# A four-layer encoder trunk whose transposed activations move to another place in each partition's memory

## The chip, the cores and the metric

The kernel runs on one core of one Trainium2 chip. The metric is the device time of one execution in microseconds: lower is better. Before the change the median of three runs is 2669.81 us (2667.91 to 2669.83).

## The reference

A trunk of four post-norm layers over a sequence of 512 tokens of width 1,024. Each layer is a token mixer and a dense feed-forward network (FFN), each followed by a layer norm of `alpha * x + y`. The mixers alternate: multi-head latent attention (MLA) in layers 0 and 3, retention in layer 1, gated linear attention (GLA) in layer 2.

```python
def swiglu_ffn(x, w_in, w_out):
    gate, up = jnp.split(x @ w_in, 2, axis=-1)
    return (jax.nn.silu(gate) * up) @ w_out

for i in range(DEPTH):                       # DEPTH = 4
    y = (mla_mixer, retention_mixer, gla_mixer)[i % 3](x, ...)
    x = layer_norm(DEEPNORM_ALPHA * x + y, ln_g[i, 0], ln_b[i, 0])
    x = layer_norm(DEEPNORM_ALPHA * x + swiglu_ffn(x, ffn_w_in[i], ffn_w_out[i]), ln_g[i, 1], ln_b[i, 1])
```

Everything is float32. `w_in` of the FFN is 1,024 x 5,632 and `w_out` 2,816 x 1,024, so nearly all work is in products of the activations with weights that are read once.

## The kernel before

**A product is three matmuls.** Every operand is kept as two parts, high and low (`split`, lines 99 to 102: ScalarE copies the high part in the rounded type fp32r, VectorE subtracts to get the low part). `mm3` (lines 124 to 128) then issues hi x hi, hi x lo and lo x hi into one accumulator in PSUM. In `mm(out, s, m)` the first operand `s` is stationary (128 x 128, loaded into the array ahead of the matmul) and the second `m` is moving (up to 512 columns). The profile names both, the moving one first: `ps<-xh,whi` streams `xh` past a block of `whi`.

**The transposed activations.** `xh` and `xl` are two tiles of 128 partitions x 8 x 512 floats (16,384 bytes in each partition), the high and low part of x with features on the partitions. `x_to_xT` (lines 151 to 161) fills them from the activations `xt` by TensorE transposes; in MLA the attention's output is put into them too (line 576). They live for the whole program. They are the moving operand where the result has features on the partitions (FFN in, retention's queries and keys, GLA's queries and keys: `proj_f`, line 261) and the stationary operand where it has tokens there (`proj_tile`, line 281, and MLA's output projection, line 616).

**The weights.** `wload` (line 104) brings 512 KB at a time into one of three `wraw` buffers on SyncE's queue; `wsplit` makes `whi` and `wlo` of it, six buffers each of 4,096 bytes per partition.

**All other operands** are blocks of 2,048 bytes per partition from a pool that each mixer and each FFN opens for itself (`phase`, line 76; tags `b`, `v`, `r`). In FFN out and in retention's and GLA's output projections they are stationary and the weights move (`ps<-whi,bh`); in retention's and GLA's inner products both operands come from this pool (`ps<-bh,bl`).

**Where things lie.** Pools are laid out one behind the other in the order in which they are opened, and the tiles in a pool in the order in which they are first asked for, each padded to a multiple of 32 bytes. Each partition of the built program before has, in bytes from its start:

| what | from | to |
|---|---|---|
| DMA scratch and four constants | 0 | 1,152 |
| `cp`: `ident` | 1,152 | 1,664 |
| `cp`: `xh` | 1,664 | 18,048 |
| `cp`: `xl` | 18,048 | 34,432 |
| `cp`: `xt` (four), rotary tables | 34,432 | 55,040 |
| `wp`: `wraw` (three) | 55,040 | 67,328 |
| `wp`: `whi` (six) | 67,328 | 91,904 |
| `wp`: `wlo` (six) | 91,904 | 116,480 |
| `sp`, `lnp` | 116,480 | 125,696 |
| `phase` | 125,696 | 223,136 |

In the GLA mixer's phase a 32-byte tile (`ba`, line 853) stands behind the 35 blocks of tag `b`, so the blocks of tags `v` that follow begin at 197,408.

The framework's planner sets the order of instructions on each engine from the program text, its dependences and its own costs (`issue_after` and `keep_in_program_order` pin a few places); a pool that rotates its buffers makes an instruction wait until the last reader of the buffer is done. The 12 matmuls that close a run of GLA scores are the first of the state updates (line 1092): their moving operand is `v`, a block of tag `v`, and the profile calls it `bh` or `bl` too.

Of the kernel before, what the change touches and what calls it, by code (L numbers as in the profile page):

```python
# [10 lines left out]
F32R = mybir.dt.float32r  # L11
# [5 lines left out]
P = 128  # L17
D = 1024
S = 512
NT = S // P  # L20
KT = D // P
# [29 lines left out]
class Trunk:  # L51
    def __init__(self, tc, ctx, ins, nb=47, nraw=3, nhl=6):
        self.tc, self.nc, self.ins = tc, tc.nc, ins
        nc = tc.nc
        ctx.enter_context(nc.allow_non_contiguous_dma(reason="rows of weights and broadcasts"))
        pool = lambda name, bufs, **k: ctx.enter_context(tc.tile_pool(name=name, bufs=bufs, **k))
        self.cp = pool("cp", 1)
        self.wp = pool("wp", 1)
        self.nb = nb
        self.sp = pool("sp", 8)  # L60
        self.lnp = pool("lnp", 2)
        self.ps_pool = pool("psum", 6, space=bass.MemoryType.PSUM)
        self.nraw, self.nhl = nraw, nhl
        self.relieve = 0
        self.pending = []
        self.waiting = []

        self.ident = self.cp.tile([P, P], F32, name="ident")
        make_identity(nc, self.ident)
        self.xh = self.cp.tile([P, KT, S], F32R, name="xh")  # L70
        self.xl = self.cp.tile([P, KT, S], F32R, name="xl")
        self.xt = [self.cp.tile([P, D], F32, name=f"xt{t}") for t in range(NT)]


# [1118 lines left out]
```

## Time and profile before

| | |
|---|---|
| median of three runs | 2669.81 us |
| the profiled execution | 2668.85 us |
| its span (first to last instruction) | 2667.1 us |
| TensorE matmuls: busy, share, number | 2611.8 us, 98%, 12,996 |
| VectorE | 1416.6 us, 53% |
| ScalarE | 906.0 us, 34% |
| DMA: moved, mean busy share of 16 engines | 230 MB, 28.5% |
| granted TensorE clock, mean | 0.994 of 2.4 GHz |

The busy time of TensorE is the union of its matmuls; they are pipelined, so that two overlap, and a matmul's own duration (some 390 ns for 512 columns) is longer than the distance from its start to the next one's start. How fast TensorE works is read from the starts.

### The profile page before, as it was taken

To read this page: it belongs to the slowest core of one execution; us is meant where nothing else is said; L and a number is where in the kernel's file an instruction comes from. 1 tells how busy PE (TensorE), PEld (TensorE's weight loads), DVE (VectorE), ACT (ScalarE), POOL (GpSimd) and SP (SyncE) were. 2 spreads that over 40 slices of the span, in tenths; PEclk is the share of its full clock that TensorE was granted. 3 is DMA by queue.
4 is the path that set the end of the run, shared out by engine and by line. 5 is a ranking of instruction groups with operands and counts; after the bars stand their busy time and mean duration, and the time that the engine had idled before them with its cause. 6 is when DMAs were issued, how large, how long until landed. Compare 5 with 4: busy or idle time off the path is not lost.

```text
span 2667.1 us, 32309 instructions
## 1 busy us (share of the span) xinstructions
PE 2611.8 (98%) x12996; PEld 2191.9 (82%) x12996; DVE 1416.6 (53%) x2484; ACT 906.0 (34%) x1381; POOL 218.7 (8%) x231
## 2 busy tenths in 40 slices
PE   8999999999999999999999999999999999999998
PEld 6888888887888888888888998888888788888886
DVE  6878433238755548333226888833335586633334
ACT  4752322213333332322213654322212564322211
POOL 3002000001110103000002010100002200100001
PEclk9999999999999999999999999999999999999999
DMA  4212433232223222333223221333322221333321
GB/s 142 72 40 68 127 95 95 95 95 87 79 72 95 88 93 82 103 95 95 95 94 99 75 64 56 107 95 95 95 95 78 67 74 48 101 93 94 94 95 56
DMA packets 294711, 232.35 MB, mean 87 GB/s; under 512 B 21120, under 2 KB 244480, under 8 KB 294560
## 3 DMA queue, kind: packets, MB, share of 16 engines
q1 hardware_dynamic: 294560, 230.28, 28.5%
q8 instruction: 102, 1.67, 0.3%
q14 instruction: 49, 0.40, 0.0%
HBM read 228.15 MB, written 2.10 MB: 86 GB/s over the span
## 4 chain that ended last, share of the span: by engine, by line
PE 84%; DVE 10%; POOL 2%; issue 2%; ACT 2%; DMA 1%; DVEq 0%; SPq 0%; ACTq 0%; POOLq 0%
PE ps L126 27%; PE ps L128 27%; PE ps L127 27%; DVE xt L203 2%; DVE xt L204 1%; PE tp L555 1%; DVE lnst L184 1%; DVE xl L101 1%; PE ps L536 1%; DVE lnu L143 1%; PE ps L535 1%; DVE xt L182 1%; DMA wraw<-in_mla_w_down 0%; PE tp L156 0%; DVE bl L101 0%
## 5 line engine op out<-in xcount | busy, mean ns | idle before, releaser
L100 ACT CAST whi<-wraw 128x1024 fp32r<-128x1024 f32 (+3 forms) x414 | 430.4, 1040 | 1150.9 <-issue 383.9
L101 DVE TENSOR_TENSOR wlo<-wraw,whi 128x1024 fp32r<-128x1024 f32 (+2 forms) x366 | 444.4, 1215 | 674.5 <-ACT whi L100 664.1
L127 PE MATMUL ps<-xl,whi 128*128 128x512 f32 (+1 forms) x1792 | 666.0, 372 | 8.5 <-DVE xl L101 8.5
L126 PE MATMUL ps<-xh,whi 128*128 128x512 f32 (+1 forms) x1792 | 666.3, 372 | 0.0
L128 PE MATMUL ps<-xh,wlo 128*128 128x512 f32 (+1 forms) x1792 | 665.5, 371 | 0.0
L127 PEld LDWEIGHTS ps<-xl,whi 128*128 128x128 f32 x1792 | 338.6, 189 | 72.5 <-DVE xl L101 9.7
L126 PEld LDWEIGHTS ps<-xh,whi 128*128 128x128 f32 x1792 | 338.7, 189 | 63.1 <-issue 0.4
L128 PEld LDWEIGHTS ps<-xh,wlo 128*128 128x128 f32 x1792 | 338.5, 189 | 62.9
L126 PE MATMUL ps<-whi,bh 128*128 128x512 f32 (+1 forms) x960 | 369.4, 385 | 0.2 <-ACT bh L100 0.2
L128 PE MATMUL ps<-whi,bl 128*128 128x512 f32 (+1 forms) x960 | 368.0, 383 | 0.0
L127 PE MATMUL ps<-wlo,bh 128*128 128x512 f32 (+1 forms) x960 | 367.8, 383 | 0.0
L128 PE MATMUL ps<-whi,xl 128*128 128x512 f32 (+3 forms) x752 | 264.8, 352 | 5.3 <-DVE xl L101 5.3
L126 PE MATMUL ps<-whi,xh 128*128 128x512 f32 (+3 forms) x752 | 267.0, 355 | 0.8 <-ACT xh L100 0.8
L127 PE MATMUL ps<-wlo,xh 128*128 128x512 f32 (+3 forms) x752 | 264.3, 351 | 0.1
L101 POOL TENSOR_TENSOR wlo<-wraw,whi 128x1024 fp32r<-128x1024 f32 (+4 forms) x48 | 117.3, 2457 | 1672.1 <-ACT whi L100 1658.8
L126 PEld LDWEIGHTS ps<-whi,bh 128*128 128x128 f32 x960 | 181.0, 189 | 35.6 <-ACT bh L100 1.0
L128 PEld LDWEIGHTS ps<-whi,bl 128*128 128x128 f32 x960 | 180.9, 188 | 35.5 <-DVE bl L101 0.6
L127 PEld LDWEIGHTS ps<-wlo,bh 128*128 128x128 f32 x960 | 180.9, 188 | 34.7
L304 DVE TENSOR_TENSOR b<-ps,b 128x512 f32<-128x512 f32 x88 | 60.9, 692 | 273.5 <-PE ps L128 272.8
L128 PEld LDWEIGHTS ps<-whi,xl 128*128 128x128 f32 x752 | 142.3, 189 | 25.5 <-DVE xl L101 6.6
L126 PEld LDWEIGHTS ps<-whi,xh 128*128 128x128 f32 x752 | 142.5, 189 | 20.5 <-ACT xh L100 1.2
L127 PEld LDWEIGHTS ps<-wlo,xh 128*128 128x128 f32 x752 | 142.6, 190 | 19.0 <-POOL wlo L101 0.4
(220 smaller groups left out, 2780.4 us busy)
## 6 DMA issues: line engine op xcount, KB each, us to landing
wraw<-in_ffn_w_in SPq DMA_DIRECT2D x176, 512.0 KB, 3.8
wraw<-in_ffn_w_out SPq DMA_DIRECT2D x88, 512.0 KB, 3.3
wraw<-in_ret_w_in SPq DMA_DIRECT2D x48, 512.0 KB, 3.8
wraw<-in_gla_w_in SPq DMA_DIRECT2D x22, 512.0 KB, 3.6
wraw<-in_mla_w_o SPq DMA_DIRECT2D x16, 512.0 KB, 3.8
wraw<-in_ret_w_o SPq DMA_DIRECT2D x16, 512.0 KB, 4.8
wraw<-in_mla_w_down SPq DMA_DIRECT2D x8, 512.0 KB, 4.5
wraw<-in_mla_w_ukv SPq DMA_DIRECT2D x8, 512.0 KB, 3.7
```

The costliest lines, as they stand in the source:

```text
L100: a = self.nc.scalar.copy(hi, src)
L101: b = (eng or self.nc.vector).tensor_tensor(lo, src, hi.bitcast(F32), op=ALU.subtract)
L126: mm(out, s[0], m[0], start=start, stop=False)
L127: mm(out, s[0], m[1], start=False, stop=False)
L128: mm(out, s[1], m[0], start=False, stop=stop)
L143: stt(u, y, y, x, op0=ALU.mult, op1=ALU.mult)
L182: nc.vector.scalar_tensor_tensor(x, x, coef, ps, op0=ALU.mult, op1=ALU.add)
L184: nc.vector.bn_stats(self.stats[t][:, half * 6 : half * 6 + 6], x)
L203: nc.vector.scalar_tensor_tensor(x[:, sl], x[:, sl], mv[:, 0:1], self.g[:, sl], op0=ALU.subtract, op1=ALU.mult)
L204: nc.vector.scalar_tensor_tensor(x[:, sl], x[:, sl], r, self.bb[:, sl], op0=ALU.mult, op1=ALU.add)
L304: nc.vector.tensor_tensor(s, pu, s, op=ALU.mult)
L535: nc.tensor.matmul(ps, qr[:, sl], krh, start=False, stop=False)
```

## The change

The two tiles `xh` and `xl` are no longer taken from the pool `cp`, the first that is opened, but from a pool of their own, `xp`, which is opened behind `wp`, `sp` and `lnp` and ahead of the phases' pools. Nothing else in the program text differs.

```diff
@@ Trunk.__init__
         self.sp = pool("sp", 8)
         self.lnp = pool("lnp", 2)
+
+        xp = pool("xp", 1)
+        self.xh = xp.tile([P, KT, S], F32R, name="xh")
+        self.xl = xp.tile([P, KT, S], F32R, name="xl")
         self.ps_pool = pool("psum", 6, space=bass.MemoryType.PSUM)
@@
         make_identity(nc, self.ident)
-        self.xh = self.cp.tile([P, KT, S], F32R, name="xh")
-        self.xl = self.cp.tile([P, KT, S], F32R, name="xl")
         self.xt = [self.cp.tile([P, D], F32, name=f"xt{t}") for t in range(NT)]
```

By the same rule of layout, everything between `xl` and the phases moves down by 32,768 bytes and the two tiles move up by 91,264: `xt` from 1,664, `wraw` from 22,272, `whi` from 34,560 to 59,136, `wlo` from 59,136 to 83,712, `sp` and `lnp` to 92,928, `xh` from 92,928, `xl` from 109,312. The phases' pools begin at 125,696 as before.

## Rows read from the trace of the kernel before

**Rows 1.** The page: busy time of each engine; the chain that ended last, by engine.
```profile
PE 2611.8 (98%) x12996; PEld 2191.9 (82%) x12996; DVE 1416.6 (53%) x2484; ACT 906.0 (34%) x1381; POOL 218.7 (8%) x231
...
PE 84%; DVE 10%; POOL 2%; issue 2%; ACT 2%; DMA 1%; DVEq 0%; SPq 0%; ACTq 0%; POOLq 0%
```

**Rows 2.** Busy time by stretch: start of MLA, FFN in, FFN out of layer 0.
```profile
core 0: us, PE busy (x) PEld busy (x) DVE busy (x) ACT busy (x) POOL busy (x), PEclk, DMA share, GB/s
0.00:60.00 60.00, 50.81 (x263) 43.75 (x263) 35.74 (x59) 27.94 (x57) 23.63 (x67) 1.00 0.51 158
...
263.00:478.00 215.00, 215.00 (x996) 177.52 (x996) 82.98 (x97) 66.87 (x85) 0.00 (x0) 1.00 0.35 103
478.00:600.00 122.00, 122.00 (x538) 100.77 (x538) 35.10 (x45) 23.75 (x24) 4.79 (x2) 1.00 0.30 95
```

**Rows 3.** Matmuls by start and duration (us), FFN in, layer 0: first, 173rd.
```profile
299.81 0.40 PE L128 MATMUL ps<-xh,wlo 128*128 128x512 f32 x1
...
339.79 0.39 PE L126 MATMUL ps<-xh,whi 128*128 128x512 f32 x1
```

**Rows 4.** The same view, FFN in of layer 1: first and 173rd.
```profile
1119.68 0.40 PE L128 MATMUL ps<-xh,wlo 128*128 128x512 f32 x1
...
1159.82 0.40 PE L126 MATMUL ps<-xh,whi 128*128 128x512 f32 x1
```

**Rows 5.** The same view, FFN out of layer 0: first and 178th.
```profile
499.70 0.39 PE L128 MATMUL ps<-whi,bl 128*128 128x512 f32 x1
...
539.82 0.39 PE L128 MATMUL ps<-whi,bl 128*128 128x512 f32 x1
```

**Rows 6.** The same view, retention, both operands of the phase's pool: first, 16th.
```profile
999.72 0.39 PE L128 MATMUL ps<-bh,bl 128*128 128x512 f32 x1
...
1003.12 0.39 PE L128 MATMUL ps<-bh,bl 128*128 128x512 f32 x1
```

**Rows 7.** Matmuls by start, GLA scores: first, 22nd, 34th (the first not of them).
```profile
1628.44 0.28 PE L126 MATMUL ps<-bh 128*128 128x256 f32 x1
...
1630.96 0.28 PE L126 MATMUL ps<-bh 128*128 128x256 f32 x1
...
1632.38 0.40 PE L126 MATMUL ps<-whi,bh 128*128 128x512 f32 x1
```

**Rows 8.** The same view, a GLA projection of 256 columns: first and 40th.
```profile
1614.65 0.28 PE L127 MATMUL ps<-wlo,xh 128*128 128x256 f32 x1
...
1619.27 0.28 PE L127 MATMUL ps<-wlo,xh 128*128 128x256 f32 x1
```

**Rows 9.** Groups by shape (count, busy us, mean ns): 512 columns, by operands.
```profile
L126 PE MATMUL ps<-xh,whi 128*128 128x512 f32 x1408 | 556.0, 395 | 0.0
...
L126 PE MATMUL ps<-whi,bh 128*128 128x512 f32 x896 | 350.6, 391 | 0.2 <-ACT bh L100 0.2
...
L126 PE MATMUL ps<-whi,xh 128*128 128x512 f32 x432 | 172.7, 400 | 0.0
...
L126 PE MATMUL ps<-bh,whi 128*128 128x512 f32 x128 | 51.9, 409 | 0.7 <-ACT bh L434 0.7
...
L126 PE MATMUL ps<-bh,xh 128*128 128x512 f32 x16 | 6.5, 405 | 0.0
```

**Rows 10.** Groups by shape: 256 and 320 columns with `xh`.
```profile
L126 PE MATMUL ps<-xh,whi 128*128 128x256 f32 x384 | 110.3, 287 | 0.0
...
L126 PE MATMUL ps<-whi,xh 128*128 128x256 f32 x224 | 63.8, 285 | 0.0
...
L126 PE MATMUL ps<-whi,xh 128*128 128x320 f32 x64 | 21.1, 330 | 0.8 <-ACT xh L100 0.8
```

**Rows 11.** Transposes by start, eight merged: of `xt`, and of a block of MLA's phase.
```profile
608.94 1.04 PE L156 MATMUL tp<-ident,xt 128*128 128x128 f32 x8
...
180.02 1.03 PE L555 MATMUL tp<-ident,b 128*128 128x128 f32 x8
```

## The prediction

> **What bounds the kernel now.** I read the page first, for which engine sets the end. Matmuls are busy for 2,611.8 of 2,667.1 us, and the chain that ended last is TensorE's to 84% [rows 1]; the next engine, VectorE, is at 53%. So the time is the number of matmuls times the distance from one start to the next, plus a few gaps. Then the stretches: in FFN in and FFN out the matmuls fill all of the 215 and 122 us at a full clock (PEclk 1.00), with DMA busy 0.35 and 0.30, VectorE 83 and 35 us, ScalarE 67 and 24 us [rows 2]. Only the first 60 us leave TensorE idle (50.8 busy).
>
> Nothing is added or removed here, so the one thing to ask is whether a matmul's pace depends on where its operands lie. For that I read starts in the time-ordered view, kind by kind:
> - FFN in, layer 0 (`xh` and `xl` move past weights): 172 steps in 39.98 us, 232.4 ns each [rows 3]. Layer 1: 172 steps in 40.14 us, 233.4 ns [rows 4].
> - FFN out (weights move past blocks of the phase's pool): 177 steps in 40.12 us, 226.7 ns [rows 5].
> - Retention with both operands in the phase's pool: 15 steps in 3.40 us, 226.7 ns [rows 6].
>
> All four have 512 columns, 128 x 128 stationary blocks, and one PSUM bank as target. FFN in and FFN out also bring and split weights at the same rate (24 matmuls to a 512 KB load). What sets the first two apart is the pair `xh`, `xl`, and its place.
>
> **Why the place, and which property of it.** From the table of the layout, take each address modulo 256. `whi`, `wlo` and all blocks of tag `b` begin at a multiple of 256 (67,328 = 263 x 256; 91,904 = 359 x 256; 125,696 = 491 x 256), and so does each row and each slice that these matmuls read. `xh` and `xl` begin 128 behind one (1,664 = 6 x 256 + 128; 18,048 = 70 x 256 + 128). The kernel holds one more case of that sort, far from the start of memory: GLA's `v`, at 197,408 = 771 x 256 + 32. In one run of GLA scores, 21 steps of 256 columns with all operands on multiples take 2.52 us, 120.0 ns each; then the moving operand becomes `v`, and 12 steps take 1.42 us, 118.3 ns [rows 7]. The projections with `xh` at 256 columns step by 4.62 us / 39 = 118.5 ns [rows 8]. So operands off the multiple share a pace that is not the aligned one, whether they lie at 1,664 or at 197,408: 1.5 ns quicker at 256 columns, 6 to 7 ns slower at 512. I take the offset as the cause.
>
> **The change part by part.** `xh` goes to 92,928 = 363 x 256 and `xl` to 109,312 = 427 x 256. Modulo 2,048 both are then 768, as blocks of tag `b` are; and the weights shift by 32,768, which leaves their offsets alone. So each matmul with `xh` or `xl` becomes, in its offsets, one of those that run at 226.7 ns today.
>
> - *512 columns.* There are 3 x (1,408 + 432 + 16) = 5,568 (one of the three lines of `mm3` stands for each kind [rows 9]). The mean of the two paces is 232.9 ns, so 6.24 ns each: -34.7 us. This is what all of them would give.
> - *Runs that don't settle.* The whole of FFN out, with its starts, takes 122.0 us for some 536 matmuls, 227.5 ns, 0.8 above the settled 226.7 [rows 2, 5]. FFN in is one run of 912 a layer, 3,648 in all; the other 1,920 come in short runs, and I charge these the 0.8: +1.5 us.
> - *256 columns.* 3 x (384 + 224) = 1,824 [rows 10], from 118.5 to 120.0 ns [rows 7, 8]: +2.7 us.
> - *320 and 288 columns.* 192 [rows 10] and, from the code, 96. No row shows them with all operands aligned. By the nearest rows they lie between 1.5 ns slower (as 256) and 6.24 quicker (as 512): +0.4 to -1.8 us. I take 0, since the widths lie near 256.
> - *Gain that waits swallow.* At the head of MLA, TensorE waits for weights (9.2 of 60 us idle [rows 2]). The 192 matmuls of the query projection stand there in layers 0 and 3: up to 192 x 6.24 = 1.2 us lost.
> - *Other engines.* ScalarE and VectorE write `xh` and `xl`, DMA writes `wraw`: all at new addresses. The trace has no pair to price this, but cover is large: in FFN in they are busy for 67 and 83 of 215 us, DMA for 0.35 [rows 2]. FFN in shortened by 3% asks 3% more of them. If the cover were gone the gain of that stretch would be lost, nothing more.
> - *Transposes* read `ident` and `xt`. Both are 128 off the multiple and stay so: 0.
>
> Sum: -34.7 + 1.5 + 2.7 + 1.2 = -29.3 us. From the profiled execution's 2,668.85 us that is 2,639.5; it lies 0.96 below the median of the runs, so about 2,640.5 us.
>
> **The Trainium skill speaks against this.** The rows say that the pace goes with the operand's place: 232.4 and 233.4 against 226.7 ns [rows 3 to 5]. The page "SBUF — State Buffer", section "Who interferes with whom", gives TensorE two independent read ports of its own and says that TensorE never waits on anyone; contention exists on VectorE's and GpSimd's shared pair alone. By that rule the home of an operand would be indifferent and the sum 0. The trace does not contradict that no other engine is the disturber, but the two paces need some reason.
>
> **The rivals.**
> 1. *The place is indifferent; it is the use that is slow.* Then `xh` and `xl` keep 232.9 ns wherever they lie: 2,669.8 us. For it: all slow 512-column matmuls have `xh` or `xl`, so use and place cannot be parted at that width. The Trainium skill's page would have it so. Against: as stationary or moving operand, `xh` has the same shape and strides in use as a block of the phase's pool, and `v`, which is not `xh`, leaves the 120.0 ns too [rows 7]. Chance 0.08.
> 2. *The low end of memory is slow, and it reaches past the weights' new home.* `xh` lay below 34,432. If that is why, and the slow part ended before 34,560, the result is my forecast. But reads by TensorE of 34,560 to 67,328 are shown today for transposes alone. Were all of that slow, `whi` (34,560 to 59,136) and two of six `wlo` buffers (to 67,328) would be in it: 2/3 + 1/3 x 1/3 = 7/9 of all products with a weight. FFN in and the like would keep 7/9 of their 34.7 us and gain 7.7; the other 3 x (896 + 128) = 3,072 matmuls with weights [rows 9] would lose 6.24 x 7/9 each, 14.9 us: +7.2 us, 2,677 us. It turns into a loss from a border near 58,000, where `whi` is nearly all inside. Against: eight transposes of `xt`, which lies there now, take 1.04 us, eight of a block of the phase's pool 1.03 [rows 11], and `v` is odd at 197,408. Chance 0.05.
> 3. *Only long runs settle.* If short runs stay uneven, 3,648 x 6.24 = 22.8 us are gained and the four FFNs' 1,152 matmuls of 256 columns lose 1.7: -21 us, 2,649 us. For it: MLA's and GLA's matmuls switch width every few. Against: the short retention run is at 226.7 [rows 6]. Chance 0.08.
>
> **How the numbers follow.** Forecast 0.79, rivals 0.08, 0.05, 0.08. A measurement of this kernel tells some 0.2%, 5.3 us, from no change. Faster: forecast and rival 3, 0.87; within: rival 1, 0.08; slower: rival 2, 0.05. Low end: the full 34.7 us without the losses, 2,634. High end: beyond rival 3 by its own 3 us, 2,652; that leaves out rivals 1 and 2 and some of the forecast's tail.
>
> **What would show it.** Right: FFN in's steps at 226.7 ns in all four layers, the same as FFN out's, unchanged; the 256-column projections at 120.0; `v` still at 118.3; 12,996 matmuls, order as before. Wrong: steps of 232 with `xh` at 92,928 (rival 1); FFN out at over 227 ns, or `ps<-xh,whi` slower than `ps<-xh,wlo` (rival 2); FFN in at 226.7 but retention and MLA not (rival 3). If the planner orders instructions otherwise, the difference is not the place's alone.

## The result, and the profile after

The changed kernel takes 2636.39 us, the median of four runs (2635.14 to 2637.76), against 2668.86 us for four runs of the kernel before (2667.69 to 2669.83): a ratio of 0.988, 95% interval 0.986 to 0.990. It is 32.5 us faster; the forecast was 2640.5 us, 2634 to 2652.

The instructions are the same 32,309, and all but the waits for semaphores, of which a few are recorded some places earlier or later, stand in the same order on every engine; only addresses differ (line numbers are 2 higher behind the edit). So the two traces can be laid side by side row for row. First the page of the changed kernel: TensorE's busy time fell by 33 us, VectorE's and ScalarE's by under 1 us, and the chain is still TensorE's.

```profile
PE 2578.4 (98%) x12996; PEld 2191.5 (83%) x12996; DVE 1416.0 (54%) x2484; ACT 905.5 (34%) x1381; POOL 220.6 (8%) x231
...
PE 85%; DVE 9%; POOL 2%; issue 2%; ACT 2%; DMA 1%; DVEq 0%; SPq 0%; ACTq 0%; POOLq 0%
```

Then the starts, in the time-ordered view (start and duration in us, line, operation, target, moving operand, stationary operand). FFN in of layer 0: the 1st and the 179th matmul of the stretch, 178 steps in 40.34 us, 226.6 ns each, against 232.4 [rows 3].

```profile
299.63 0.39 PE L128 MATMUL ps<-xh,whi 128*128 128x512 f32 x1
...
339.97 0.39 PE L129 MATMUL ps<-xl,whi 128*128 128x512 f32 x1
```

FFN in of layer 1, from 1,109.76 to 1,149.88 us: 177 steps, 226.7 ns, against 233.4 [rows 4]; the table below has all four layers.

FFN out of layer 0: 177 steps in 40.12 us, 226.7 ns, as in [rows 5].

```profile
499.77 0.39 PE L129 MATMUL ps<-wlo,bh 128*128 128x512 f32 x1
...
539.89 0.39 PE L129 MATMUL ps<-wlo,bh 128*128 128x512 f32 x1
```

A GLA projection of 256 columns: 38 steps in 4.56 us, 120.0 ns, against 118.5 [rows 8]. (GLA's `v`, which still lies 32 bytes off, has 11 steps from 1,612.28 to 1,613.57 us, 117.3 ns, against 118.3 [rows 7].)

```profile
1599.83 0.28 PE L128 MATMUL ps<-whi,xh 128*128 128x256 f32 x1
...
1604.39 0.28 PE L130 MATMUL ps<-whi,xl 128*128 128x256 f32 x1
```

The time from the first of FFN in's 912 long-run matmuls to the first of FFN out, read from such starts, and the stretches between, in us (MLA, retention, GLA and MLA each end with the FFN's first matmuls of 256 columns):

| stretch | before | after | difference |
|---|---|---|---|
| MLA, layer 0 | 275.6 | 274.6 | -1.0 |
| FFN in, layer 0 | 211.9 | 206.8 | -5.2 |
| FFN out and retention | 600.9 | 595.7 | -5.2 |
| FFN in, layer 1 | 212.8 | 206.8 | -6.1 |
| FFN out and GLA | 415.0 | 411.6 | -3.5 |
| FFN in, layer 2 | 211.9 | 206.8 | -5.2 |
| FFN out and MLA, layer 3 | 391.1 | 389.3 | -1.8 |
| FFN in, layer 3 | 212.8 | 206.8 | -6.1 |
| FFN out, layer 3 | 119.5 | 119.5 | 0.0 |

FFN in's differences are the change's alone. The stretches with mixers also hold waits on VectorE, and behind a wait TensorE's granted clock sometimes falls for a while from 2.4 to 1.2 GHz. In the stretch of FFN out and GLA TensorE's three longest waits stand at the same places in both kernels: 2.0, 2.3 and 3.6 us before, 1.8, 2.3 and 3.6 us after. What the clock was just behind each of them (columns as in [rows 2]; PEclk is the third figure from the end), before:

```profile
1624.20:1627.20 3.00, 3.00 (x14) 3.00 (x15) 2.88 (x3) 2.98 (x6) 0.00 (x0) 0.50 0.01 3
1651.40:1654.40 3.00, 3.00 (x10) 2.31 (x9) 2.89 (x15) 0.00 (x0) 0.00 (x0) 0.50 0.22 65
1689.00:1692.00 3.00, 3.00 (x16) 3.00 (x15) 2.93 (x10) 0.99 (x2) 0.00 (x0) 0.50 0.14 51
```

and after:

```profile
1606.50:1609.50 3.00, 3.00 (x25) 2.82 (x26) 2.88 (x4) 2.98 (x6) 0.00 (x0) 1.00 0.01 3
1632.00:1635.00 3.00, 3.00 (x17) 2.32 (x16) 2.93 (x19) 0.00 (x0) 0.00 (x0) 1.00 0.39 115
1668.00:1671.00 3.00, 3.00 (x16) 2.92 (x15) 3.00 (x10) 1.17 (x2) 0.00 (x0) 0.50 0.04 5
```

So the clock fell three times before and once after, behind the same waits. Other executions of this stretch, whose places and paces are told further down, show what this is worth: with one fall it takes 411.9 us at the old paces (the pair high and 128 off) and 411.6 or 411.5 at the new ones, with two falls 413.2 at the new ones, with three 415.0 at the old ones. A fall costs some 1.6 us, and of the 3.5 us of this row 0.3 are the change's.

### The profile page after: what moved, and what is told of

Its sections match the earlier page's. It is cut to its first block, busy times and chain, and to the rows that moved or that the text cites. A ratio compares the mean times of both kernels' runs of the same rounds, so it can differ in the third digit from the quotient of the medians.

```text
span 2633.3 us, 32309 instructions
## 1 busy us (share of the span) xinstructions
PE 2578.4 (98%) x12996; PEld 2191.5 (83%) x12996; DVE 1416.0 (54%) x2484; ACT 905.5 (34%) x1381; POOL 220.6 (8%) x231
## 4 chain that ended last, share of the span: by engine, by line
PE 85%; DVE 9%; POOL 2%; issue 2%; ACT 2%; DMA 1%; DVEq 0%; SPq 0%; ACTq 0%; POOLq 0%
PE ps L128 27%; PE ps L130 27%; PE ps L129 27%; DVE xt L205 2%; DVE xt L206 1%; PE tp L557 1%; DVE lnst L186 1%; DVE xl L103 1%; PE ps L538 1%; DVE lnu L145 1%; PE ps L537 1%; DMA wraw<-in_mla_w_down 0%; DVE xt L184 0%; PE tp L158 0%; DVE bl L103 0%
## 5 line engine op out<-in xcount | busy, mean ns | idle before, releaser
L129 PEld LDWEIGHTS ps<-wlo,bh 128*128 128x128 f32 x960 | 180.5, 188 | 34.7
```

The source lines that it names most:

```text
L129: mm(out, s[0], m[1], start=False, stop=False)
```

## The experiments

**Low in memory, but on a multiple of 256.** The kernel before, with one padding tile of 128 bytes on either side of the pair (the `memset` writes its first element).

```diff
+        self.pad0 = self.cp.tile([P, 32], F32, name="pad0")
+        nc.gpsimd.memset(self.pad0[:, :1], 0.0)
         self.xh = self.cp.tile([P, KT, S], F32R, name="xh")
         self.xl = self.cp.tile([P, KT, S], F32R, name="xl")
+        self.pad1 = self.cp.tile([P, 32], F32, name="pad1")
+        nc.gpsimd.memset(self.pad1[:, :1], 0.0)
```

> The kernel before with 128 bytes of padding ahead of xh and 128 behind xl: the pair stays at the low end of memory (1,792 to 34,560) but begins at a multiple of 256; weights and blocks move up by 256 and stay on multiples. If the offset within 256 bytes is the cause: FFN in at 226.7 ns a step, 2636 to 2638 us, as after the change. If the low end of memory is slow: FFN in stays at 232 to 233 ns, 2669 us.

Measured 2640.08 us (2638.31 to 2640.79), ratio 0.989 (0.987 to 0.991). `xh` and `xl` lie at 1,792 to 34,560, and FFN in steps by 40.12 us / 177 = 226.7 ns:

```profile
299.80 0.39 PE L132 MATMUL ps<-xh,wlo 128*128 128x512 f32 x1
...
339.92 0.39 PE L132 MATMUL ps<-xh,wlo 128*128 128x512 f32 x1
```

The low end of memory is not slow: 256 bytes of padding in the old place give FFN in the pace that the move gives it. The whole is 2 us above the 2638 us at which the expectation ended; what makes them was not separated (the next two runs with agreeing operands, on the same chip, took 2637.6 and 2638.0).

**High in memory, but 128 off.** The changed kernel with the same padding around the pair, in `xp`.

```diff
         xp = pool("xp", 1)
+        self.pad0 = xp.tile([P, 32], F32, name="pad0")
+        nc.gpsimd.memset(self.pad0[:, :1], 0.0)
         self.xh = xp.tile([P, KT, S], F32R, name="xh")
         self.xl = xp.tile([P, KT, S], F32R, name="xl")
+        self.pad1 = xp.tile([P, 32], F32, name="pad1")
+        nc.gpsimd.memset(self.pad1[:, :1], 0.0)
```

> The changed kernel with 128 bytes of padding ahead of xh and 128 behind xl: the pair keeps its new home (93,056) but begins 128 bytes behind a multiple of 256, as it did in its old one. Offset theory: FFN in back at 232 to 233 ns a step, 2668 to 2670 us, the whole gain gone. Low-end theory: FFN in at 226.7 ns, 2636 us.

Measured 2669.26 us (2665.80 to 2670.93, ten runs), ratio 0.9996 (0.9987 to 1.0005): the whole gain is gone. FFN in of layer 0 steps by 40.13 us / 172 = 233.3 ns:

```profile
299.81 0.40 PE L132 MATMUL ps<-xh,whi 128*128 128x512 f32 x1
...
339.94 0.40 PE L133 MATMUL ps<-xl,whi 128*128 128x512 f32 x1
```

So the home behind the weights is worth nothing by itself that these runs could tell.

**Everything 128 off.** The kernel before with one padding tile, behind `xl`: the weights (67,456) and the phases' blocks (125,824) now begin 128 bytes behind a multiple of 256, as `xh` and `xl` do.

```diff
         self.xl = self.cp.tile([P, KT, S], F32R, name="xl")
+        self.pad1 = self.cp.tile([P, 32], F32, name="pad1")
+        nc.gpsimd.memset(self.pad1[:, :1], 0.0)
```

> The kernel before with 128 bytes of padding behind xl: now xh, xl, all weights and all blocks of the phases begin 128 bytes behind a multiple of 256 (only v and the transposes' xt differ). If what counts is the distance of an operand from a multiple: all 512-column matmuls at 232 to 233 ns, FFN out too; 3,680 more of them at 6.24 ns, so some 2690 us. If what counts is that the two operands of a matmul differ in their offset: all at 226.7, 2637 us. Low-end theory: as before, 2669 us.

Measured 2637.61 us (2636.72 to 2640.61), ratio 0.988 (0.987 to 0.990). FFN in: 178 steps in 40.35 us, 226.7 ns; FFN out: 177 in 40.12, 226.7 ns.

```profile
299.62 0.39 PE L129 MATMUL ps<-xl,whi 128*128 128x512 f32 x1
...
339.97 0.39 PE L130 MATMUL ps<-xh,wlo 128*128 128x512 f32 x1
...
499.77 0.39 PE L130 MATMUL ps<-whi,bl 128*128 128x512 f32 x1
...
539.89 0.39 PE L130 MATMUL ps<-whi,bl 128*128 128x512 f32 x1
```

This falls against the reason that the prediction gave. No operand need lie on a multiple of 256; the operands need only agree in their distance from one. `xh` and `xl` were slow because they differed from everything that they met.

**256 off.** The changed kernel with 256 bytes ahead of `xh` (the pair and the phases on multiples of 512, the weights 256 behind one).

> The changed kernel with 256 bytes of padding ahead of xh: the pair and the phases' blocks lie at multiples of 512, the weights 256 behind one. If 256 is the step that counts: 2636 us, FFN in and FFN out at 226.7 ns. If it is 512: both FFN in and FFN out mix two offsets (or have one operand off) and step at about 232 to 233 ns, some 2669 to 2690 us.

Measured 2638.01 us (2635.85 to 2641.05), ratio 0.988 (0.987 to 0.990). FFN in steps by 226.7 ns (177 in 40.12 us), so a distance of 256 between the operands is as good as none.

```profile
299.74 0.39 PE L132 MATMUL ps<-xh,wlo 128*128 128x512 f32 x1
...
339.86 0.39 PE L132 MATMUL ps<-xh,wlo 128*128 128x512 f32 x1
```

**The cost by itself.** Behind the changed kernel stand runs of 61 matmuls on one tile of 10,240 floats, in a phase of their own.

```diff
...
+        mv = lambda k, d, n: big[:, (k % 8) * 512 + d // 4 : (k % 8) * 512 + d // 4 + n]
+        st = lambda k, d: big[:, 6144 + (k % 16) * 128 + d // 4 : 6144 + (k % 16) * 128 + d // 4 + P]
+        for name, n, pairs in self.CASES:
+            ps = self.ps_pool.tile([P, 512], F32, tag="ps", name=name)
+            for k in range(self.STEPS):
+                dm, ds = pairs[k % len(pairs)]
+                nc.tensor.matmul(ps[:, :n], st(k, ds), mv(k, dm, n), start=k == 0, stop=k == self.STEPS - 1)
...
+    STEPS = 61
```

> The changed kernel, and behind it 25 runs of 61 matmuls each on one tile of the phase's pool, 128 x 128 stationary blocks; each run fixes how far the moving and the stationary operand begin behind a multiple of 256 bytes. Only the steps between starts in these runs are read. Theory (the two operands of a matmul must agree modulo 256, which the run with all operands 128 off suggests): 226.7 ns at 512 columns for differences 0, 256 and 512 and for both 128 off; 232 to 233 ns for 32, 64, 96, 128, 160, 192, 224, whichever operand is off; 120.0 ns against 118.5 at 256 columns. Rival: what must agree is the moving operand with the stationary block that is loaded for the next matmul while it streams. Two runs part them: alternating pairs (0, 0), (128, 128) agree within each matmul and differ across; pairs (0, 128), (128, 0) differ within and agree across. Theory: 226.7 in the first, 232 to 233 in the second. Rival: the other way round.

The time-ordered view merges each run into one row, under its target's name; the difference of two starts, over 61, is the step. In `s_a` to `s_j` the stationary operand is 0, 32, 64, 96, 128, 160, 192, 224, 256, 512 bytes off; in `m_b` both are 128 off; `x_a` alternates (0, 0) and (128, 128), `x_b` (0, 128) and (128, 0); in `m_a` the moving operand alone is 128 off.

```profile
2648.80 14.00 PE L1169 MATMUL s_a<-probe 128*128 128x512 f32 x61
2662.63 14.39 PE L1169 MATMUL s_b<-probe 128*128 128x512 f32 x61
2676.86 14.40 PE L1169 MATMUL s_c<-probe 128*128 128x512 f32 x61
2691.10 14.44 PE L1169 MATMUL s_d<-probe 128*128 128x512 f32 x61
2705.37 14.33 PE L1169 MATMUL s_e<-probe 128*128 128x512 f32 x61
2719.55 14.40 PE L1169 MATMUL s_f<-probe 128*128 128x512 f32 x61
2733.78 14.14 PE L1169 MATMUL s_g<-probe 128*128 128x512 f32 x61
2747.76 14.39 PE L1169 MATMUL s_h<-probe 128*128 128x512 f32 x61
2761.99 13.99 PE L1169 MATMUL s_i<-probe 128*128 128x512 f32 x61
2775.82 13.99 PE L1169 MATMUL s_j<-probe 128*128 128x512 f32 x61
2789.64 14.38 PE L1169 MATMUL m_a<-probe 128*128 128x512 f32 x61
2803.86 14.02 PE L1169 MATMUL m_b<-probe 128*128 128x512 f32 x61
2817.72 14.10 PE L1169 MATMUL x_a<-probe 128*128 128x512 f32 x61
2831.66 14.19 PE L1169 MATMUL x_b<-probe 128*128 128x512 f32 x61
2845.69 6.92 PE L1169 MATMUL w_as<-probe 128*128 128x128 f32 x61
```

`s_a`, `s_i` and `s_j` step by 13.83 us / 61 = 226.7 ns, `m_b` by 227.2 (its start included). The differences between step by 229.2 (192 off, `s_g`) to 233.9 ns (96 off, `s_d`), and `m_a` by 233.1. So the theory of the agreement modulo 256 holds for constant pairs. On which pair must agree neither view holds: `x_a`, which agrees within each matmul, steps by 228.5 ns, `x_b`, which agrees across, by 230.0. Both cost something, and each less than the constant difference of 128 (`s_e`, 232.5). By the same division (rows not shown) 256 columns give 120.7 ns agreeing and 118.9 with 128 off, 320 columns 146.9 and 146.7, 384 columns 173.4 and 175.9.

**Only `xl` off.** The changed kernel with a padding tile of 128 bytes between `xh` and `xl` and one behind: one of the three matmuls of each product with `xh` and `xl` has operands that differ.

> The changed kernel with 128 bytes of padding between xh and xl and 128 behind xl: xh lies on a multiple of 256 as the weights and blocks do, xl 128 behind one. One of the three matmuls of each product then has operands that differ. If each such matmul costs some 6.2 ns by itself: a third of the 5,568, 11 us of the gain are lost, 2647 us. If a single difference upsets the pace of the whole run: FFN in at 232 to 233 ns and 2668 us. If it is absorbed by its two neighbours: 2637 us.

Measured 2658.91 us (2654.18 to 2662.94), ratio 0.996 (0.995 to 0.998): some two thirds of the gain are lost to a third of the matmuls, between the first two answers, so that none of the three was right. FFN in of layer 0 has the full 233.3 ns (172 steps in 40.13 us); in layer 2 it steps by 40.28 us / 176 = 228.9, with the same addresses and order (in layer 1 by 231.1 and in layer 3 by 233.3; each layer keeps its pace from its first matmul to its last):

```profile
299.81 0.40 PE L133 MATMUL ps<-xl,whi 128*128 128x512 f32 x1
...
339.94 0.39 PE L134 MATMUL ps<-xh,wlo 128*128 128x512 f32 x1
...
1739.63 0.39 PE L134 MATMUL ps<-xh,wlo 128*128 128x512 f32 x1
...
1779.91 0.40 PE L133 MATMUL ps<-xl,whi 128*128 128x512 f32 x1
```

**Mixed runs.** The same set-up with other patterns.

> The changed kernel, and behind it 24 runs of 61 matmuls on one tile, as in the run before; only steps between starts are read. Open from it: alternating pairs that agree within a matmul and differ across stepped by 228.4 ns, those that differ within and agree across by 230.0, and a third of differing matmuls took two thirds of the gain. Theory A (two costs that add, 3.3 ns where a matmul's own operands differ and 1.7 where the moving one and the next stationary differ): every second matmul with an operand 128 off gives 226.7 + 2.5 = 229.2, one in three 228.4, one in six 227.5, one in twelve 227.1; pairs that change every second matmul and agree within, 227.5. Theory B (a difference upsets a rhythm that needs some six agreeing matmuls to settle): one in two, three and six all at 230 to 233, one in twelve some 228.5 to 230; agreeing pairs that change every sixth matmul above 228. Runs of 256 columns with differences of 32 to 224: between 118 and 120 ns if they share one cause with 128; a step under 117 would point to a placement that is better still.

`y_b`, `y_c`, `y_d`, `y_e`: the moving operand 128 off in every second, third, sixth, twelfth matmul, the rest agreeing; `y_a`: the stationary one in every second; `z_a` and `z_b`: agreeing pairs that change every second and every sixth. `q_a` and `q_b`: 256 columns, the stationary operand 32 and 64 off.

```profile
2648.35 14.39 PE L1169 MATMUL y_a<-probe 128*128 128x512 f32 x61
2662.58 14.19 PE L1169 MATMUL y_b<-probe 128*128 128x512 f32 x61
2676.61 14.12 PE L1169 MATMUL y_c<-probe 128*128 128x512 f32 x61
2690.57 14.05 PE L1169 MATMUL y_d<-probe 128*128 128x512 f32 x61
2704.46 14.02 PE L1169 MATMUL y_e<-probe 128*128 128x512 f32 x61
2718.32 14.29 PE L1169 MATMUL z_a<-probe 128*128 128x512 f32 x61
2732.45 14.09 PE L1169 MATMUL z_b<-probe 128*128 128x512 f32 x61
2746.37 14.30 PE L1169 MATMUL z_c<-probe 128*128 128x512 f32 x61
...
2767.72 7.08 PE L1169 MATMUL q_b<-probe 128*128 128x256 f32 x61
2774.64 7.49 PE L1169 MATMUL q_c<-probe 128*128 128x256 f32 x61
```

`y_b` to `y_e` step by 230.0, 228.9, 227.7, 227.2 ns, near theory A; but `y_a` has 233.3 where A says 229.2, and `z_a` 231.6 where A says 227.5. Theory B says 230 to 233 for one in three and one in six, and misses those, though `z_b` is at 228.2, as it foresaw. Both fall. In `y_b` to `y_e` the excess over 226.7 comes to 6 to 7 ns for each matmul whose moving operand is off, with nothing for the others; one stationary operand off (`y_a`) costs twice that. The pairs that change (`x_a`, `x_b`, `z_a`, `z_b`) follow neither figure. `y_c` is the pattern of the run with `xl` off, which in layer 2 had the same 228.9, but in layer 0 233.3. What picks among the paces is not settled.

Five runs (rows not shown) have the moving operand off by itself. 64 off (start 2,825.09, next start 2,839.07) it steps by 229.2 ns, as the stationary one does 192 off; 160 off (2,839.07 to 2,853.34) by 233.9, as the stationary one does 96 off. So what counts is how far the one lies ahead of the other modulo 256.

`q_b` is a find: 6.92 us / 61 = 113.4 ns at 256 columns. The six other differences there give 117.7 to 120.0.

**A placement that might be better still.** The weight buffers are 4,352 bytes each, and a load can begin some bytes into its own. The FFNs' first weights begin 64 in; in the second kernel GLA's of 256 columns begin 192 in as well. A third run repeats the changed kernel on the same chip. The lines that hand the distance down to the buffers are left out here.

```diff
...
-            wg = self.wcols(w_in, 0, KT, f * P, P)
-            wu = self.wcols(w_in, 0, KT, F + f * P, P)
+            wg = self.wcols(w_in, 0, KT, f * P, P, 64)
+            wu = self.wcols(w_in, 0, KT, F + f * P, P, 64)
...
-            ws = [self.proj_w(w, c0, 256, 4) for _, c0, _ in parts]
+            ws = [self.proj_w(w, c0, 256, 4, off=192) for _, c0, _ in parts]
...
-            wv, wr, n = self.proj_w(w, cv, 256, 4), [], 256 + 2 * GLA_RANK
+            wv, wr, n = self.proj_w(w, cv, 256, 4, off=192), [], 256 + 2 * GLA_RANK
```

> The changed kernel once more, beside the two that build on it, so that the three share their runs of the kernel before: 2636 us, give or take 2.

> The changed kernel with weight buffers of 4,352 bytes, and the weights of each FFN's first three blocks of features begin 64 bytes into theirs. They are the stationary operands of 1,152 matmuls of 256 columns whose moving operand stays on a multiple of 256. If the 113.3 ns of the run on one tile hold here against 120.0: 6.7 ns each, 7.7 us at most, less what TensorE then waits for the layer norm before it: 2629 to 2633 us. If the 113.3 ns hang on the single tile or the steady run: 2636 us.

> As the one before, and GLA's weights of 256 columns begin 192 bytes into their buffers: there the weights move and xh, xl are stationary, so that the stationary operand again lies 64 bytes ahead of the moving one modulo 256. 672 more matmuls of 256 columns, 4.5 us at most: 2624 to 2631 us in all if the difference alone decides, 2629 to 2633 if only weights as stationary operand gain.

Measured 2638.28 us for the changed kernel (2636.36 to 2640.49; ratio to before 0.989, 0.987 to 0.991), 2636.03 with the FFNs' weights moved (2633.76 to 2636.80; 0.988, 0.986 to 0.989), 2634.99 with GLA's too (2634.71 to 2635.08; 0.988, 0.986 to 0.989). The steps did what was hoped: in the last kernel 38 steps of a GLA projection take 4.30 us, 113.2 ns.

```profile
1488.40 0.28 PE L131 MATMUL ps<-whi,xh 128*128 128x256 f32 x1
...
1492.70 0.28 PE L133 MATMUL ps<-whi,xl 128*128 128x256 f32 x1
```

But the time did not follow. In the stretch from 1,400 to 1,700 us TensorE's waits are alike to 0.1 us but for one (us in total, times, longest), which in the repeat of the changed kernel reads

```profile
PE tp L1052 <- DVE bl L103: 1.8, 1, 1.8
```

and in the kernel with both:

```profile
PE tp L1055 <- DVE bl L103: 5.0, 3, 3.0
```

The transposes of GLA's keys wait for VectorE 3.2 us longer: TensorE arrives earlier at work that is not ready. The stretch from FFN out to the next FFN in takes 413.2 us in the one and 413.5 in the other. The clock has a part in that: behind the three longest waits of this stretch it fell twice in the first and three times in the second (1.00, 0.52, 0.53 and 0.50, 0.50, 0.51 of 2.4 GHz over 3 us), which is worth some 1.6 us. The longer wait need not be behind the third fall: with the FFNs' weights alone moved, where that wait is 1.8 us as in the first, the clock fell three times too (0.51, 0.51, 0.50). Both expectations that foresaw a gain of 5 us or more missed; the intervals of the three ratios overlap, so that a gain of 3 us is not shown, though all four runs of the last kernel (2635.08 us at most) lie below all four of the changed one (2636.36 at least).

## Why the prediction was right, point by point

**What bounds the kernel** held: with the order unchanged, a quicker step on TensorE became time almost one for one.

**Which property of the place** was right for the sum and wrong in its wording. "So operands off the multiple share a pace that is not the aligned one": the run with everything 128 off shows that being off is harmless. `v` was at 32 against operands at 0, so it fitted both readings, and the text took the narrower one. The step that carried the sum, that each matmul with `xh` becomes one whose operands stand to each other as in [rows 5], was the sound one.

**512 columns, with the runs that don't settle: -34.7 + 1.5 = -33.2 us forecast.** Over all such matmuls whose distance to the next start is under 255 ns (5,523 before, 5,522 after), the mean above 226.7 ns fell from 6.1 to 0.2 ns: about -32.6 us. FFN in alone gave 5.2 + 6.1 + 5.2 + 6.1 = 22.5 us; forecast 3,648 x 6.24 ns = 22.8.

**256 columns: +2.7 us forecast.** Over those whose distance is under 150 ns (1,760 before, 1,731 after) the mean lies 1.1 ns below 120.0 before and 0.1 after: +1.8 us. The term was too large, since the mean before was 118.9 ns and not the 118.5 of the one run that was read.

**320 and 288 columns: 0 taken.** At 320 columns, agreeing and 128 off, the runs by themselves step by 146.9 and 146.7 ns; in the kernels the steps of 288 columns have a mean of 133.1 ns before and 132.6 after, which for 96 is nothing.

**Gain that waits swallow: +1.2 us forecast.** This is the mis-sized term: no stretch shows a loss. MLA of layer 0 got 1.0 us shorter, though the clock fell once there (0.50 from 241.2 to 244.2 us) and not at all before, and FFN out with MLA of layer 3 got 1.8 shorter, where 288 matmuls x 6.24 less 288 x 1.5 would give 1.4 each. GLA's 192 wide matmuls give 1.2 us and its 960 narrow ones take back up to 1.4; the 3.5 us by which that stretch got shorter are the clock's but for 0.3, as told beside the table.

**The sum.** The terms as measured, -32.6 and +1.8, make -30.8 us. The median fell by 32.5. The 1.7 us between are no term of the prediction; runs of one kernel differ by 2 to 3 us, and the profiled execution before had the clock down more often than the one after in the stretch with GLA. What part of the 1.7 us the clock has in the median is not shown.

**The rivals.** That the place is indifferent and the use is slow: fell with FFN in at 226.7 ns. In the first runs on one tile no other engine worked at all (the row below, columns as in [rows 2]: VectorE, ScalarE and GpSimd 0.00 us), and the pace of 512 columns lay between 226.7 and 233.9 ns by how the two operands lie to each other. The Trainium skill's page "SBUF — State Buffer", section "Who interferes with whom", from which that rival followed, gives TensorE two independent read ports and says that TensorE never waits on anyone. The trace agrees in so far as no other engine is needed for the slow pace; it does not bear out that the place of the two operands is indifferent. That the low end is slow: fell with the padded kernel before, 2640 us. That only long runs settle: fell, since retention and FFN out took 5.2 us less together, and 6.0 less in the repeat of the changed kernel (594.9), where 1,152 x 6.24 less 288 x 1.5 ns make 6.8.

```profile
2650.00:2940.00 290.00, 288.07 (x1460) 249.52 (x1458) 0.00 (x0) 0.00 (x0) 0.00 (x0) 1.00 0.00 1
```

## What to carry to other kernels

Read the steps between matmul starts by kind of operand, not the busy share: 98% busy held 32 us that a shift of 128 bytes gave back. Where two kinds of the same shape step differently, look at how their operands lie to each other modulo 256 bytes, and test it with a padding tile before anything is moved. What lies ahead of a large tile sets its distance (here the 1,152 bytes of DMA scratch and constants, 4.5 x 256; the identity's 512 bytes leave it as it is), so pad there. This is shown for 512 columns and 128 x 128 stationary blocks in fp32r; at 256 columns agreement was the slower one. Before a difference of a few us between two executions is put down to a change, compare the granted clock behind each wait.

## What was not expected

- What counts at 512 columns is the difference of the two operands' distances modulo 256 bytes: 226.7 ns at 0, 256 and 512, 229.2 to 233.9 ns at the seven multiples of 32 between.
- At 256 columns agreement is not the best: 120.0 ns settled, 118.5 at 128 off, 113.4 with the stationary operand 64 bytes ahead. At 320 columns, agreeing and 128 off are alike.
- A differing run has several paces. With the same addresses and instructions FFN in of the kernel before had 232.4 ns in layer 0 and 233.4 in layer 1; with only `xl` off it had 233.3, 231.1 and 228.9. A run that agrees throughout had one pace in every kernel here. Why a difference costs, and what chooses the pace, no run here shows.
- Behind the same waits of TensorE the clock falls to 1.2 GHz in one execution and not in the next: three falls against one made 3.1 of the 3.5 us by which two executions of the stretch with GLA differ. What decides it no run here shows.
